# Later route exponentials, freed conditioning steps in the odd mixer, and three u tiles' activations kept in their buffers and used first

## The chip, the cores and the metric

The kernel runs on one core of one Trainium2 chip. The metric is the device time of one execution in microseconds (us). Three runs of the kernel before took 2802.61, 2803.46 and 2820.34 us; their median is 2803.46 us. One further execution was profiled, and all rows below come from it.

The engines are TensorE (PE in the profile; PEld is its weight load), VectorE (DVE), ScalarE (ACT), GpSimd (POOL) and SyncE (SP). DMAs are issued from the queues of SP and ACT.

## The reference, cut to what matters

A first block (stick-breaking attention and a mixture of experts) is followed by two layers of a second block. Layer 0 has the even mixer, layer 1 the odd one; both end in a PEER feed-forward over 16384 single-neuron experts. There are 256 tokens of width 1024.

```python
for layer in range(2):
    mod = (c_act @ ada_w[layer] + ada_b[layer])[:, None, :]
    sh1, sc1, g1, sh2, sc2, g2 = jnp.split(mod, 6, axis=-1)
    h = rmsnorm(x, norm_mix[layer]) * (1.0 + sc1) + sh1
    y = even_mixer(h, ...) if layer % 2 == 0 else odd_mixer(h, ...)
    x = x + g1 * y
    h = rmsnorm(x, norm_ffn[layer]) * (1.0 + sc2) + sh2
    x = x + g2 * peer_ffn(h, ...)

def odd_mixer(h, w_in, b_forget, w_out):          # 16 heads of 64
    q, k, v, f = split_cols(h @ w_in, ODD_SIZES)
    return forgetting_attention(q, k, v, f + b_forget) @ w_out

def peer_ffn(h, w_q, sub_keys, u, v):
    q = (ht @ w_q).reshape(T, 8, 2, 128)
    s = jnp.einsum('thpd,pnd->thpn', q, sub_keys)
    top_s, top_i = lax.top_k(s, 16)
    cand_s = top_s[:, :, 0, :, None] + top_s[:, :, 1, None, :]
    best_s, best_j = lax.top_k(cand_s.reshape(T, 8, -1), 16)
    experts = ...                                  # one of 128 * 128 per pick
    gates = jax.nn.softmax(best_s, axis=-1)
    act = jax.nn.gelu(jnp.einsum('cd,ced->ce', xc, u[ec]))
    return jnp.einsum('ce,ced->cd', gc * act, v[ec])
```

## The kernel before

The kernel doesn't gather experts. In `peer` it multiplies the hidden state with all 16384 rows of u, in 128 tiles of 128 experts (the first product), builds a dense gate matrix G of 128 x 128 x 256, and multiplies the gated activations with all rows of v, again in 128 tiles (the second product). Every fp32 operand is split into a high part (cast by ACT, line 175) and a remainder (subtracted by DVE, line 179, or by POOL, line 181), and each product is three matmuls (`mm3`, lines 216 to 218).

**A u tile** (`act_tile`, with `stream` of line 1261) streams 512 KB of weights in, splits two halves of 512 columns (`puh`, `pul`, three buffers each), runs 24 matmuls into a PSUM bank `u`, and applies the gelu on ACT (line 1273) into a tile `peerA`, of which there are three buffers. `tiles(n)` (line 1278) runs the next n of the 128 tiles and stores each to device memory (`spill`, line 1282, on ACT's queue).

**Routing** (`peer_route`) finds the top 16 per head on DVE, for two halves of the tokens: a long series of maximum and index instructions, then the subtraction of the best score (line 1205), index arithmetic (lines 1208 to 1216), and after the exponentials on ACT (line 1218) the normalisation (lines 1220 to 1222). `tiles(N_EXP)` stands ahead of the exponentials, with N_EXP = 23, and these are ordered behind the last of those gelus by `after(..., k.gelu)`; gelu and exponential use different ACT function tables. `tiles(N_TR)`, with N_TR = 7, stands between normalisation and the transposes (line 1227), which are ordered behind the last of its matmuls. These 30 tiles take their remainders on POOL. The other 98 tiles run among the 64 steps that build G (lines 1294 to 1305) with remainders on DVE.

**The second product** loops over the 128 tiles: it loads the activations back (`get`, line 1310, two tiles ahead), multiplies them with G on DVE (line 1333), splits the result (`pwh`, `pwl`) and the v tile (`pvh`, `pvl`, and `puh`, `pul` for the second half), and accumulates into four PSUM banks `o`. Eight tiles before its end it loads the residual (`xin` into the buffer of `hh`, line 1322).

**Conditioning.** `ada_vec` computes one sixth of a modulation vector as a generator. A step loads part of the weights (`ada` on SP's queue, 1 MB, or `pada` on ACT's queue, 256 KB) and accumulates on DVE (lines 301 and 305). After two steps of the 1 MB kind half a vector is complete; the next step flushes it (`ada_end`: four DVE operations of line 318 for a row, and matmuls of line 325 or 322). `advance(k, n)` runs n steps, `advance(k)` all that are left. In the mixers `load_split` runs `k.bgn` steps, 1 here, each time it fetches a weight block. The odd mixer fetches 13 blocks of `od_in`: one for the forget gate, then for each of four groups of heads q, k and v (`heads`, `heads`, `rows`), and four of `od_out`. Three vectors, twelve steps, belong to it. With `hold=k.norm` the first accumulation of each half vector is ordered behind the norm ahead of the mixer.

The order of instructions on each engine is set when the program is built, by a list scheduler that runs on modelled times: an instruction that is ready in the model while its engine is free can be put ahead of earlier code. At run time every engine takes its instructions in that fixed order.

Of the kernel before, what the change touches and what calls it, by code (L numbers as in the profile page):

```python
# [21 lines left out]
P = 128  # L22
T = 256
# [10 lines left out]
CAP = 64  # L34
EC = 4
EV_QI, EV_KI, EV_CKV, EV_QA, EV_QB, EV_KB, EV_VB = 0, 512, 640, 904, 1416, 1928, 2440
NT = 128
N_EXP, N_TR = 23, 7

CONST = ["anti", "ge", "cum", "m_sb", "m_c"]  # L40
SMALL = [("ident", P), ("iota", P), ("one", P), ("strict", P), ("c1", 8), ("c2", 8), ("ng0", 8), ("ng1", 8), ("nm0", 8), ("nm1", 8),
# [210 lines left out]
class Ahead:  # L252
# [15 lines left out]
    def get(self):  # L268
        if not self.q:
            self.fill()  # L270
        return self.q.popleft()
# [803 lines left out]
def odd_mixer(k, gate):  # L1075
# [3 lines left out]
    with k.tc.tile_pool(name="od", bufs=2, side="right") as pool:  # L1079
# [11 lines left out]
        def rows(g):  # L1091
            proj_rows(k, w, 2 * D + g * 256, 256, v[:, :, g * 256:(g + 1) * 256])
# [24 lines left out]
        nc.vector.tensor_copy(cT, pt[:16, :T])  # L1117
        nc.sync.dma_start(kT[64:65], cT)
        rows(0)
        oT = [one([P, 8, T], f"od_oT{i}", F32R) for i in range(2)]  # L1120
        po = [None]
        for g in range(4):
# [118 lines left out]
def peer(k, l):  # L1241

    nc, a = k.nc, k.a
    spill = k.dram.tile([NT, P, T], F32, name=f"peer_a{l}")
    outer = ExitStack()
    k.pp = outer.enter_context(banks(k, f"p{l}", u=2, o=4))
    acc = [[bank(k, "o") for n in range(2)] for th in range(2)]
    with k.tc.tile_pool(name=f"peer{l}", bufs=2) as pool, k.tc.tile_pool(name=f"pws{l}", bufs=4) as wp:
# [24 lines left out]
            k.gelu = nc.scalar.activation(A, ps[:, :T], AF.Gelu_apprx_tanh)  # L1273
            return A

        left = iter(range(NT))

        def tiles(n, **kw):
            for _ in range(n):
                i = next(left, None)  # L1280
                if i is not None:
                    nc.scalar.dma_start(spill[i], act_tile(i, **kw))

        peer_route(k, l, idx, gates, tiles)
        k.pst.close()
        with k.tc.tile_pool(name=f"peerg{l}", bufs=1, side="right") as gpool:
            G = gpool.tile([P, NT, T], F32, name=f"G{l}")
            rest = NT - N_EXP - N_TR
            for t4 in range(T // 4):
                tiles((t4 + 1) * rest * 4 // T - t4 * rest * 4 // T, lo_eng="dve")  # L1290
                t0 = 4 * t4

                oh = tmp(k, pool, [P, 4, 2, P // 2, 2], "oh", BF16, tag="pvl", bufs=3)
                nc.vector.tensor_tensor(oh.rearrange("p t c i d -> p (t c) i d"), iob[:, None].to_broadcast([P, 8, P // 2, 2]),
                                        idx[:, t0:t0 + 4].rearrange("p t c d -> p (t c) d")[:, :, None, :].to_broadcast([P, 8, P // 2, 2]),
                                        ALU.is_equal)
                og = [tmp(k, pool, [P, 4, P // 2, 2], "og", BF16, tag=g, bufs=3) for g in ("pvh", "pwh", "pwl")]
                for c in range(3):
                    nc.vector.tensor_tensor(og[c], oh[:, :, 0], gates[:, t4, c, :, None, :].to_broadcast([P, 4, P // 2, 2]), ALU.mult)
                pg = bank(k).rearrange("p (t i) -> p t i", t=4)  # L1300
                for j in range(4):
                    for c in range(3):
                        nc.tensor.matmul(pg[:, j], oh[:, j, 1].rearrange("p i d -> p (i d)"), og[c][:, j].rearrange("p i d -> p (i d)"),  # L1303
                                         start=j == 0 and c == 0, stop=True, skip_group_check=True)
                nc.scalar.copy(G[:, :, t0:t0 + 4], pg.rearrange("p t i -> p i t"))
            tiles(NT)

            def get(i):
                A = tmp(k, pool, [P, T], "peerA", bufs=3)
                nc.sync.dma_start(A, spill[i])  # L1310
                return A

            As, vs = deque(), deque()

            xin = k.hh.bitcast(F32).rearrange("p (h c) t -> p h (c t)", h=2)
            gate, k.gb = (k.hl.bitcast(F32)[:, 4 * j:4 * j + 4, :].rearrange("p c t -> p (c t)") for j in range(2))
            for i in range(NT):
                advance(k, 1 - i % 2 if k.bg else 1)
                if i == NT - 8:
                    k.set, k.users = None, [k.gelu]  # L1320
                    preload(k, SETS[AF.Ln])
                    nc.sync.dma_start(xin, k.xd)
                    nc.sync.dma_start(gate, k.gd[l])
                    if l:
                        nc.sync.dma_start(k.gb, k.nfd[0, :].partition_broadcast(P))
                while len(As) < 3 and i + len(As) < NT:
                    As.append(get(i + len(As)))
                    vs.append(stream(a[f"pv{l}"][i + len(vs)]))
                ahead.fill()
                A, v = As.popleft(), vs.popleft()  # L1330

                w = bank(k, "u")[:, :T]
                nc.vector.tensor_mul(w, A, G[:, i, :])
                wh, wl = split(k, pool, w, "pw", bufs=3)
                for n in range(2):

                    vp = split(k, pool, v[:, n * 512:(n + 1) * 512], "pu" if n else "pv", bufs=3)
                    for th in range(2):
                        ts = slice(th * P, (th + 1) * P)
                        mm3(k, acc[th][n], (wh[:, ts], wl[:, ts]), vp, i == 0)  # L1340
            advance(k)
    open_x(k, l + 1)
    if l == 0:
# [44 lines left out]
def program(k, out):  # L1388
# [52 lines left out]
    for l in range(2):  # L1441
        mod = k.mod[l + 1]
        with Section(k, f"m{l}", (4, 6)[l], "right", s=3, t=1, o=2):
# [4 lines left out]
                with norm("m1", "right") as k.nw:  # L1448
                    norm_T(k, k.nm1, mod[:, 8:16], mod[:, 0:8], "s")

            k.bg = [ada_vec(k, l + 1, v, r, hold=k.norm) for v, r in ((2, g1), (4, None), (3, None))]
            k.bgn = 1
            if l:
                nc.sync.dma_start(k.nfd, a["norm_final"][None, :])
            (even_mixer, odd_mixer)[l](k, g1)
# [73 lines left out]
```

## Time and profile before

| What | Value |
|---|---|
| median of three runs | 2803.46 us (2802.61 to 2820.34) |
| the profiled execution, device time | 2797.37 us |
| its span, first to last instruction | 2795.3 us |
| PE busy / DVE busy / ACT busy / POOL busy | 94% / 65% / 45% / 14% |
| mean granted TensorE clock | 0.972 |
| layer 0: routing and first product, second product | about 905 to 1395, 1402 to 1761 us |
| layer 1: odd mixer | about 1775 to 1925 us |
| layer 1: routing and first product, second product | about 1930 to 2422, 2428 to 2780 us |

A row of a timeline gives the start in us, the time in us, the engine, the line, the operation, the tiles written and read, and in brackets how long the engine sat idle before it and what ended that. A granted clock of 1.00 is full speed (2.4 GHz), 0.50 the lower level (1.2 GHz).

### The profile page before, as it was taken

The page shows a single profiled execution, that of the slowest core. Times are in us where ns is not written, and L with a number is a line of the kernel's source. Part 1 is how long each engine was busy: PE and PEld are TensorE (multiplying, and loading weights), DVE is VectorE, ACT ScalarE, POOL GpSimd, SP SyncE. Part 2 cuts the span into 40 slices and gives each one's busy share as a digit, 9 for nine tenths or more (in the row PEclk, how much of TensorE's full clock was granted, in tenths as well). Part 3 has the DMA queues.
Part 4 walks back from the last instruction along what each step waited for, and adds up shares of the span by engine and source line. Part 5 has one row for each costly group of instructions (what it writes and reads, how often), then busy time and mean ns, then how long its engine had stood idle before and what let it go on. Part 6 is the DMA issues. An engine that isn't in the chain of part 4 may idle for free.

```text
span 2795.3 us, 47442 instructions
## 1 busy us (share of the span) xinstructions
PE 2617.3 (94%) x17213; PEld 2138.7 (77%) x17213; DVE 1819.4 (65%) x3977; ACT 1249.5 (45%) x2527; POOL 387.0 (14%) x289
## 2 busy tenths in 40 slices
PE   7998999999798979999999999798979999899998
PEld 5873344444586979999978888688979999888886
DVE  6753111111686698777787887855798777787776
ACT  4531000000445545555545555455445555555554
POOL 2220000000234472000000000224660000000000
PEclk9899999999899999999999999899989999999999
DMA  8578999998562356666798987743356666787775
GB/s 358 217 268 353 421 421 416 419 418 369 209 256 77 123 177 195 202 197 198 220 306 258 298 257 239 292 182 110 127 169 199 198 198 200 258 267 249 242 243 162
DMA packets 208149, 696.53 MB, mean 249 GB/s; under 512 B 23143, under 2 KB 91127, under 8 KB 167588
## 3 DMA queue, kind: packets, MB, share of 16 engines
q1 hardware_dynamic: 161108, 641.51, 65.8%
q10 hardware_dynamic: 46800, 51.93, 5.5%
q8 instruction: 137, 2.24, 0.3%
q14 instruction: 104, 0.85, 0.1%
HBM read 655.55 MB, written 37.78 MB: 248 GB/s over the span
## 4 chain that ended last, share of the span: by engine, by line
PE 59%; DVE 3%; issue 2%; DMA 2%; POOL 1%; ACT 0%; SPq 0%; POOLq 0%; DVEq 0%; ACTq 0%
PE u L216 8%; PE u L218 8%; PE u L217 8%; PE o L218 7%; PE o L217 7%; PE o L216 7%; PE w L1303 3%; PE w L216 2%; PE w L217 2%; PE w L218 2%; DMA pada<-in_ada 1%; POOL pul L181 1%; DVE adaacc L305 1%; PE w L1170 1%; DMA peerA<-peer_a 1%
## 5 line engine op out<-in xcount | busy, mean ns | idle before, releaser
L216 PE MATMUL u<-hh,puh 128*128 128x256 f32 x2048 | 589.0, 288 | 24.2 <-ACT puh L175 24.2
L175 ACT CAST puh<-pst 128x512 fp32r<-128x512 f32 x768 | 476.7, 621 | 296.3 <-PE u L217 285.4
L218 PE MATMUL u<-hh,pul 128*128 128x256 f32 x2048 | 579.3, 283 | 9.4 <-POOL pul L181 9.0
L217 PE MATMUL u<-hl,puh 128*128 128x256 f32 x2048 | 577.8, 282 | 0.0
L179 DVE TENSOR_TENSOR pul<-pst,puh 128x512 fp32r<-128x512 f32 x648 | 444.7, 687 | 157.0 <-ACT puh L175 156.4
L216 PEld LDWEIGHTS u<-hh,puh 128*128 128x128 f32 x2048 | 388.8, 190 | 24.6 <-ACT puh L175 24.6
L218 PEld LDWEIGHTS u<-hh,pul 128*128 128x128 f32 x2048 | 388.1, 190 | 13.1 <-POOL pul L181 12.1
L217 PEld LDWEIGHTS u<-hl,puh 128*128 128x128 f32 x2048 | 389.1, 190 | 0.0
L175 ACT CAST pvh<-pst 128x512 fp32r<-128x512 f32 x256 | 159.2, 622 | 195.2 <-ACT puh L175 118.2
L179 DVE TENSOR_TENSOR pvl<-pst,pvh 128x512 fp32r<-128x512 f32 x256 | 176.6, 690 | 67.0 <-ACT pvh L175 67.0
L181 POOL TENSOR_TENSOR wspl<-wT,wsph 128x512 fp32r<-128x512 f32 (+1 forms) x82 | 113.5, 1386 | 746.2 <-DMA kc<-in_k_consts 492.2
L216 PE MATMUL o<-pvh,pwh 128*128 128x512 f32 x512 | 202.2, 395 | 13.8 <-ACT pwh L175 13.8
L217 PE MATMUL o<-pvl,pwh 128*128 128x512 f32 x512 | 200.9, 392 | 0.6 <-DVE pvl L179 0.5
L218 PE MATMUL o<-pvh,pwl 128*128 128x512 f32 x512 | 200.7, 393 | 0.6 <-DVE pwl L179 0.6
L216 PE MATMUL o<-puh,pwh 128*128 128x512 f32 x512 | 200.1, 391 | 0.0
L217 PE MATMUL o<-pul,pwh 128*128 128x512 f32 x512 | 200.1, 391 | 0.0
L218 PE MATMUL o<-puh,pwl 128*128 128x512 f32 x512 | 199.9, 391 | 0.0
L216 PE MATMUL w<-hh,wsph 128*128 128x256 f32 x648 | 190.9, 295 | 7.4 <-ACT wsph L175 2.9
L218 PE MATMUL w<-hh,wspl 128*128 128x256 f32 x648 | 186.5, 288 | 0.5 <-DVE wspl L179 0.5
L217 PE MATMUL w<-hl,wsph 128*128 128x256 f32 x648 | 186.7, 288 | 0.0
L181 POOL TENSOR_TENSOR pul<-pst,puh 128x512 fp32r<-128x512 f32 x120 | 172.0, 1446 | 61.3 <-ACT puh L175 54.7
L744 DVE TENSOR_TENSOR moesg<-moesg,v 128x512 f32<-128x512 f32 x16 | 11.0, 687 | 223.9 <-PE v L739 223.9
(405 smaller groups left out, 5022.8 us busy)
## 6 DMA issues: line engine op xcount, KB each, us to landing
pst<-in_pu SPq DMA_DIRECT2D x256, 512.0 KB, 4.0
pst<-in_pv SPq DMA_DIRECT2D x256, 512.0 KB, 4.6
moeg<-in_moe_g SPq DMA_DIRECT2D x64, 1024.0 KB, 10.8
moeu<-in_moe_u SPq DMA_DIRECT2D x64, 1024.0 KB, 9.9
moed<-in_moe_d SPq DMA_DIRECT2D x64, 1024.0 KB, 11.9
ada<-in_ada SPq DMA_DIRECT2D x56, 1024.0 KB, 6.7
peer_a<-peerA ACTq DMA_DIRECT2D x256, 128.0 KB, 3.6
peerA<-peer_a SPq DMA_DIRECT2D x256, 128.0 KB, 3.8
```

The costliest lines, as they stand in the source:

```text
L175: ins = nc.scalar.copy(hi, src)
L179: nc.vector.tensor_tensor(lo, src, hi, ALU.subtract)
L181: nc.gpsimd.tensor_tensor(lo, src, hi, ALU.subtract)
L216: mm(out, lhs[0], rhs[0], start=st, stop=True, skip_group_check=True)
L217: mm(out, lhs[0], rhs[1], start=False, stop=True, skip_group_check=True)
L218: k.mm = mm(out, lhs[1], rhs[0], start=False, stop=True, skip_group_check=True)
L305: nc.vector.scalar_tensor_tensor(acc, wt[:, c, :], cond[:, kc, :1], acc, op0=ALU.mult, op1=ALU.add)
L744: nc.vector.tensor_mul(sg, sg, pgu["u"])
L1170: nc.tensor.matmul(ps[:, (2 * th + p) * P:(2 * th + p + 1) * P], qh[:, p, th * P:(th + 1) * P], keys[:, p, :], start=True, stop=True)
L1303: nc.tensor.matmul(pg[:, j], oh[:, j, 1].rearrange("p i d -> p (i d)"), og[c][:, j].rearrange("p i d -> p (i d)"), start=j == 0 and c == 0 ...
```

## The change

Three things are changed. `N_EXP` goes from 23 to 28 in both layers, so that 28 tiles stand ahead of the route exponentials, 7 between them and the transposes, and 93 in the building of G. In layer 1, `k.bgn` is 0 until `rows(0)` is done and 1 from then on, and the conditioning of layer 1 is no longer ordered behind the norm (`hold=None`); layer 0 is as it was. The last three u tiles (`KEEP = 3`) are not stored: their activations stay in the three `peerA` buffers, and the second product takes these three tiles first and the other 125 after them.

```diff
-NT = 128
-N_EXP, N_TR = 23, 7
+NT, KEEP = 128, 3
+N_EXP, N_TR = 28, 7
...
         rows(0)
+        k.bgn = 1
         oT = [one([P, 8, T], f"od_oT{i}", F32R) for i in range(2)]
...
-    spill = k.dram.tile([NT, P, T], F32, name=f"peer_a{l}")
+    spill = k.dram.tile([NT - KEEP, P, T], F32, name=f"peer_a{l}")
...
-        left = iter(range(NT))
+        left, kept = iter(range(NT)), {}
 
         def tiles(n, **kw):
             for _ in range(n):
                 i = next(left, None)
-                if i is not None:
-                    nc.scalar.dma_start(spill[i], act_tile(i, **kw))
+                if i is None:
+                    return
+                A = act_tile(i, **kw)
+                if i < NT - KEEP:
+                    nc.scalar.dma_start(spill[i], A)
+                else:
+                    kept[i] = A
...
+            order = list(range(NT - KEEP, NT)) + list(range(NT - KEEP))
+
             def get(i):
+                if i in kept:
+                    return kept[i]
                 A = tmp(k, pool, [P, T], "peerA", bufs=3)
                 nc.sync.dma_start(A, spill[i])
                 return A
...
-            for i in range(NT):
-                advance(k, 1 - i % 2 if k.bg else 1)
-                if i == NT - 8:
+            for m, i in enumerate(order):
+                advance(k, 1 - m % 2 if k.bg else 1)
+                if m == NT - 8:
...
-                while len(As) < 3 and i + len(As) < NT:
-                    As.append(get(i + len(As)))
-                    vs.append(stream(a[f"pv{l}"][i + len(vs)]))
+                while len(As) < 3 and m + len(As) < NT:
+                    As.append(get(order[m + len(As)]))
+                    vs.append(stream(a[f"pv{l}"][order[m + len(vs)]]))
...
-                        mm3(k, acc[th][n], (wh[:, ts], wl[:, ts]), vp, i == 0)
+                        mm3(k, acc[th][n], (wh[:, ts], wl[:, ts]), vp, m == 0)
...
-            k.bg = [ada_vec(k, l + 1, v, r, hold=k.norm) for v, r in ((2, g1), (4, None), (3, None))]
-            k.bgn = 1
+            k.bg = [ada_vec(k, l + 1, v, r, hold=None if l else k.norm) for v, r in ((2, g1), (4, None), (3, None))]
+            k.bgn = 1 - l
```

## Rows read from the trace of the kernel before

**Rows 1.** The page, part 1: busy time of each engine over the span.

```profile
PE 2617.3 (94%) x17213; PEld 2138.7 (77%) x17213; DVE 1819.4 (65%) x3977; ACT 1249.5 (45%) x2527; POOL 387.0 (14%) x289
```

**Rows 2.** PE's waits: waiter, what for, us in total, times, longest.

```profile
PE u L216 <- ACT puh L175: 24.2, 2, 12.1
...
PE o L216 <- ACT pwh L175: 13.8, 3, 6.8
PE w L325 <- DVE adaacc L318: 11.2, 4, 9.2
```

**Rows 3.** ACT's timeline at the route exponentials of layer 0.

```profile
1028.77 0.38 ACT L1273 ACTIVATE peerA<-u 128x256 f32<-128x256 f32 x1
...
1031.61 0.38 ACT L1273 ACTIVATE peerA<-u 128x256 f32<-128x256 f32 x1
...
1047.43 0.42 ACT L1218 ACTIVATE rows<-rows 128x256 f32<-128x256 f32 x1 [14.14 <-DVE rows L1205]
...
1048.49 1.28 ACT L1273 ACT_TABLE_LOAD   x1
1049.79 0.38 ACT L1273 ACTIVATE peerA<-u 128x256 f32<-128x256 f32 x1
```

**Rows 4.** Windows: busy us and instructions by engine, PEclk, DMA share, GB/s.

```profile
1050.00:1055.00 5.00, 4.76 (x24) 4.76 (x24) 5.00 (x4) 2.14 (x6) 3.09 (x3) 0.55 0.47 159
1150.00:1200.00 50.00, 50.00 (x482) 49.58 (x482) 36.85 (x71) 28.77 (x56) 0.00 (x0) 1.00 0.64 198
```

**Rows 5.** POOL's timeline in the routing of layer 0.

```profile
972.87 61.79 POOL L181 TENSOR_TENSOR pul<-pst,puh 128x512 fp32r<-128x512 f32 x40 [7.88 <-ACT puh L175]
1048.55 1.64 POOL L181 TENSOR_TENSOR pul<-pst,puh 128x512 fp32r<-128x512 f32 x1 [13.89 <-ACT puh L175]
```

**Rows 6.** DVE's timeline in the routing of layer 0.

```profile
989.07 0.40 DVE L1203 MAX8 bv<-c 128x8 f32<-128x256 f32 x1
...
995.42 1.16 DVE L1205 TENSOR_TENSOR rows<-bv 128x128 f32<-128x128 f32 x1
...
1040.97 0.40 DVE L1203 MAX8 bv<-c 128x8 f32<-128x256 f32 x1
...
1047.12 0.27 DVE L1205 TENSOR_TENSOR rows<-bv 128x128 f32<-128x128 f32 x1
...
1063.70 1.50 DVE L1222 TENSOR_TENSOR rows<-rows,gz 128x256 f32<-128x256 f32 x1
```

**Rows 7.** The tile `rows`: duration min/median/max in ns, first and last start.

```profile
L1227 PE MATMUL w<-smalls,rows x12: 270/272/273, 1068.5 to 2095.5; 128*128 128x128 f32 x12
```

**Rows 8.** PE's timeline in the odd mixer.

```profile
1791.11 2.04 PE L325 MATMUL w<-adaacc,smalls 128*128 128x512 f32 x2 [9.22 <-DVE adaacc L318]
```

**Rows 9.** The tile `ada`, 1740 to 1930 us: durations in ns, first and last start.

```profile
L305 DVE SCALAR_TENSOR_TENSOR adaacc<-ada,cond,adaacc x42: 729/748/1789, 1778.9 to 1860.4; 128x512 f32<-128x512 f32 x42
```

**Rows 10.** Windows in the odd mixer, columns as in rows 4.

```profile
1790.00:1795.00 5.00, 3.89 (x12) 2.88 (x13) 4.86 (x13) 0.59 (x1) 0.00 (x0) 0.50 0.93 380
1875.00:1880.00 5.00, 4.96 (x39) 4.56 (x39) 1.12 (x2) 2.82 (x7) 1.85 (x2) 1.00 0.00 0
```

**Rows 11.** DVE's timeline at the start of the second product, layer 0.

```profile
1398.21 0.75 DVE L305 SCALAR_TENSOR_TENSOR adaacc<-pada,cond,adaacc 128x512 f32<-128x512 f32 x1 [3.67 <-DMA pada<-in_ada]
...
1400.59 0.75 DVE L305 SCALAR_TENSOR_TENSOR adaacc<-pada,cond,adaacc 128x512 f32<-128x512 f32 x1 [1.03 <-DMA pada<-in_ada]
1401.26 0.43 DVE L1333 TENSOR_TENSOR u<-peerA,G 128x256 f32<-128x256 f32 x1
```

**Rows 12.** ACT's timeline there: the last copy into G.

```profile
1395.83 0.58 ACT L1305 COPY G<-w 128x512 f32<-128x512 f32 x1
```

**Rows 13.** PE's timeline there: the first matmul of the second product.

```profile
1402.14 0.80 PE L216 MATMUL o<-pvh,pwh 128*128 128x512 f32 x1 [6.76 <-ACT pwh L175]
```

**Rows 14.** SP's queue there: the load of the residual.

```profile
1399.43 0.49 SPq L1322 DMA_DIRECT2D hh<-x_dram  x1
```

**Rows 15.** A window there, columns as in rows 4.

```profile
1400.00:1405.00 5.00, 2.86 (x7) 2.28 (x8) 3.79 (x8) 2.03 (x3) 0.00 (x0) 0.50 1.03 375
```

## The prediction

> **What bounds the kernel now.** I read the page first: TensorE is busy for 94% of the span [rows 1], so time is to be had only where it waits or runs at the lower clock. The view of PE's waits names three places that the change touches [rows 2]. PE waits 12.1 us in each of the two layers for a `puh` of a u tile, which ACT delivers; 6.8 us in each layer for the first `pwh` of the second product (two of the 13.8 us' three waits); and 9.2 us, once, for a conditioning row. Timelines of ACT, DVE and POOL show what lies behind each.
>
> The first is the route exponentials. Gelus come 2.84 us apart (1028.77 to 1031.61) up to the 23rd tile. The next work on ACT is the exponential, and it starts only at 1047.43, after 14.14 us of idleness that DVE's subtraction of line 1205 ended [rows 3]. ACT takes its work in order, so no further u tile can be cast; PE empties its buffers, waits, and comes back at a granted clock of 0.55 [rows 4]. The wait is for DVE's top-k, not for anything that u tiles need. While G is built PE is busy for 50.00 of 50 us, DVE for 36.85 [rows 4]: each tile taken out of that stage gives its full PE time back.
>
> **The change part by part.**
>
> *Five more tiles ahead of the exponentials, each layer.* The 28th gelu should start at 1031.61 + 5 x 2.84 = 1045.8 us and end at 1046.2; the subtraction ended at 1047.12 + 0.27 = 1047.4 [rows 3, 6]. Five tiles thus fit the gap, and the work ahead of them isn't touched. They leave the building of G, worth 5 x 2.84 = 14.2 us there. From PE's side: it gets back 12.1 us of waiting, and what the low clock cost: 24 matmuls in the window from 1050 against 5 / (2.84 / 24) = 42 at full speed, 18 x 0.118 = 2.1 us [rows 2 to 4]. Both counts give 14.2.
>
> Of this some is given back. With exponential and gelu in different tables ACT is held from about 1046.2 to the exponential's end (1047.8), and then by the next table load of 1.28 us. That is 2.9 us at least, against 1.2 us of slack that ACT has in a tile while it works beside PE (busy for 28.77 of 50 us [rows 4], so idle for 42% of 2.84). I take a wait of 1.7 us on PE. It is nothing if the three `puh` buffers cover it, and 3.3 us if the subtraction comes late, as follows.
>
> POOL was idle for 13.89 us in the gap [rows 5] and now works there. The top-k instructions don't notice: the same MAX8 takes 0.40 us with POOL busy (989.07) and idle (1040.97) [rows 5, 6]. The subtraction does: 1.16 us with POOL busy, 0.27 without [rows 6]. So the exponential comes 0.9 us later, and if the four small index operations behind it lose as much each, the normalisation of 1063.70 ends at 1063.7 + 1.5 + 4.5 = 1069.7 in place of 1065.2, an estimate. The transposes start at 1068.5 [rows 7], so they could be late by 1.2 us at most. The value: 14.2 - 1.7 = 12.5 us in each layer, 25 us in both; the bounds in a layer are 14.2 and 14.2 - 3.3 - 1.2 = 9.7. The five extra stores and loads of a tile's weights are the same transfers earlier.
>
> A switch of tables is weighed here. The second load starts at 1048.49 and the gelu at 1049.79, 1.30 us later [rows 3]: the load alone, with no gap behind it. The Trainium skill, "ScalarE: Activation LUTs", section "What ACT_TABLE_LOAD costs", counts 2.66 us for every switch, a load of 1.28 and a drain of 1.38. By that rule two switches hold ACT 2.8 us longer, and the sum would be 5.5 us smaller; the row speaks against the drain.
>
> *The odd mixer's conditioning.* Ahead of `rows(0)` four steps ran, and DVE's accumulations (0.748 us each, 42 of them on line 305 and six that open a half vector on line 301, the last at 1860 [rows 9]) crowded the first weight splits; PE waited 9.22 us for the row to be flushed [rows 8] and came back at 0.50 of the clock, with 12 matmuls in the next window [rows 10], some 12 x 0.118 = 1.4 us more than at full speed (0.118 us a matmul, as above). Without these steps in the way this is 10.6 us. The four steps are 16 accumulations, 12.0 us of DVE, and their four 1 MB loads. They don't vanish: nine steps now go with the nine fetches of groups 1 to 3, where eight went before, and three are left for `advance(k)` ahead of the output product. What hides them is DVE's idleness there: 1.12 of 5 us busy in the window from 1875, DMA share 0.00 while PE works [rows 10]. On SP's queue the weight blocks move ahead of the conditioning loads, so splits start earlier, and the last three loads stand ahead of those of `od_out`, with the idle DMA time from 1875 on to land in. If the cover weren't there, three steps would cost 3 x 4 x 0.748 = 9.0 us at PE's flush. Freeing them from the norm lets the scheduler put an accumulation into the norm's chain: 4 x 0.748 = 3.0 us for a step, or more if its load is late. I take 10.6 less 2.6 for a flush that now meets the softmax of group 0, so 8 us; bounds 10.6 and -1.4 (10.6 - 9.0 - 3.0).
>
> *The three kept tiles.* G's last copy ends at 1395.83 + 0.58 = 1396.4 [rows 12], the first matmul starts at 1402.14 [rows 13]. Of the 5.7 us between, DVE's product of 0.43 [rows 11] and a cast of about as much on ACT need at least 0.8, so at most 4.9 us can be had; the low clock adds at most half of 2.86 us, 1.4 [rows 15]. But DVE's product isn't held by the activations alone: two accumulations stand ahead of it in DVE's order, and each waited for a `pada` load, 3.67 and 1.03 us [rows 11]. Keeping the tiles takes three stores and three loads of 128 KB away, 0.79 MB, or 2.1 us at the 375 GB/s of that window [rows 15]; and it lets SP issue the 1 MB residual load of 1399.43 [rows 14] some 4 us sooner, which shares the DMA engines with the `pada` loads and could make them up to 2.8 us later. Bounds in a layer: a gain of 6.3 and a loss of 2.8. I take the nearest row, the order as it stands with less traffic: 2 us, 4 us in both. Later loads of `peerA` run two tiles ahead as before.
>
> The sum is 25 + 8 + 4 = 37 us. From the profiled execution's 2797.4 us (span 2795.3) that is 2760. The median of the runs is 6.1 us above the profiled time, and I carry that over: 2803.5 - 37 = 2766 us.
>
> **The rivals.**
>
> *Only the routing pays.* The flush meets a busy DVE in group 1, and the first product still waits for the late conditioning loads. For it: DVE's order ahead of that product holds two late loads already [rows 11]. Against it: DVE is idle most of the later odd mixer. 2803.5 - 25 = 2778 us.
>
> *Everything pays in full.* No table wait, the odd mixer's 10.6, and the product moved ahead of both accumulations: 2 x 14.2 + 10.6 + 2 x 6.3 = 51.6, so 2752 us. For it: the scheduler may place the product first, as it is ready when G is. Against it: the same scheduler put the accumulations there.
>
> *The gap doesn't fill.* The change doesn't do what it says in the routing, because POOL at work delays DVE by as much as the tiles take, and the exponential is late again. For it: 1.16 against 0.27 us [rows 6]. Against it: the MAX8s, of which the gap consists, cost the same. Left are 8 + 4 = 12 us: 2791 us.
>
> *Slower: the flush stall repeats.* Twelve steps have six flushes. If each meets DVE as the first did, now among the softmax operations, PE waits 9.22 us six times in place of once, 46 us more, against 29 gained elsewhere: 2803.5 + 17 = 2820 us. It decides from (29 + 9.2) / 6 = 6.4 us a flush on. Against it: of the four waits on line 318 in the whole kernel only one was long, 9.2 of 11.2 us [rows 2].
>
> **How the numbers follow.** The forecast has a chance of 0.55, only the routing 0.20, everything 0.12, the unfilled gap 0.09, the repeated stall 0.04. The predicted time is the forecast's, 2766. 1% of the median, about what a measurement can tell from no change, is 28 us, so faster means below 2775.4. All of "everything" lies there, nine tenths of the forecast, two fifths of "only the routing": 0.12 + 0.50 + 0.08 = 0.70. Slower by over 1% needs flushes of 11 us: 0.03. The rest, 0.27, is within 1%. The range from 2748 to 2792 takes in the first four cases and leaves out the slower one and the tails.
>
> **What would show it.** In the profile after, PE's wait for `puh` should fall from 24.2 to under 6 us, ACT's wait ahead of the exponential from 14 to under 3 us, POOL's subtractions of `pul` rise by 20 with their idle gap gone, and the building of G end some 12 us earlier against its layer's start. The odd mixer's 9.2 us wait should be gone, with later waits for lines 318 and 307 under 3 us in sum. The first matmul of the second product should follow G's last copy by 3 to 4 us in place of 5.7. The prediction is wrong if the exponential still comes late, if the norm of layer 1 gets longer by accumulations put into it, or if the waits turn up again at a flush.

## The result, and the profile after

The changed kernel took 2767.36 us (median of 4 runs, 2761.82 to 2771.66) against 2803.03 us for the kernel before on the same chip: a ratio of 0.986, with a 95% interval from 0.984 to 0.988. The prediction was 2766. The profiled execution has a span of 2760.0 us against 2795.3.

The parts don't add up as they were forecast, though. The table cuts each profiled execution at the same places. A is the time from the first score copy of a peer layer to the end of G's last copy, B from there to the first matmul of the second product, C from that matmul to the first `ybuf`, each for layers 0 / 1. D is the odd mixer's stretch, from layer 0's first `ybuf` to layer 1's first score copy. All marks are starts or ends in the timelines of ACT, PE and DVE.

| kernel | median (us) | ratio to before, interval | A | B | C | D |
|---|---|---|---|---|---|---|
| before | 2803.03 | | 480.2 / 480.1 | 5.7 / 5.8 | 357.8 / 351.6 | 182.8 |
| **changed** | 2767.36 | 0.986 [0.984, 0.988] | 469.8 / 469.0 | 1.4 / 1.4 | 354.4 / 349.8 | 184.0 |
| e1_exp28 | 2781.73 | 0.993 [0.991, 0.995] | 468.2 / 467.9 | 9.1 / 10.1 | 356.8 / 351.4 | 182.3 |
| e2_keep | 2796.73 | 0.997 [0.996, 0.999] | 481.6 / 480.7 | 1.7 / 4.1 | 355.8 / 349.6 | 183.6 |
| e3_odd | 2803.95 | 1.000 [0.999, 1.002] | 480.7 / 480.9 | 6.1 / 6.5 | 359.7 / 350.9 | 182.9 |
| e4_exp_keep | 2767.59 | 0.988 [0.986, 0.990] | 469.4 / 468.8 | 1.4 / 1.4 | 357.9 / 349.9 | 183.6 |
| e5_free | 2763.45 | 0.985 [0.981, 0.989] | 469.1 / 468.0 | 1.4 / 1.4 | 359.7 / 349.9 | 179.6 |
| e6_hold | 2763.72 | 0.985 [0.981, 0.988] | 469.3 / 468.2 | 1.4 / 1.4 | 354.4 / 350.3 | 180.9 |
| e7_nocond | 2750.41 | 0.980 [0.977, 0.983] | 468.9 / 469.3 | 1.4 / 1.4 | 357.4 / 350.3 | 167.9 |
| e8_spread | 2755.20 | 0.982 [0.978, 0.985] | 469.6 / 469.0 | 1.4 / 1.4 | 355.6 / 351.0 | 173.0 |
| e9_exp26 | 2775.70 | 0.991 [0.989, 0.992] | 474.1 / 474.0 | 1.4 / 1.4 | 354.6 / 349.9 | 184.2 |
| e10_keep1 | 2775.87 | 0.991 [0.990, 0.993] | 468.4 / 468.9 | 1.0 / 1.0 | 360.4 / 357.5 | 183.9 |
| e11_late_x | 2774.55 | 0.991 [0.988, 0.994] | 468.4 / 468.3 | 5.3 / 7.6 | 357.4 / 351.2 | 183.0 |
| e12_spread_hold | 2759.14 | 0.984 [0.983, 0.986] | 468.8 / 472.1 | 1.4 / 1.4 | 357.6 / 349.9 | 175.6 |

From before to changed, A falls by 10.5 and 11.1 us, B by 4.4 in each layer, C by 3.3 and 1.9, and D rises by 1.2. That is 34.4 us. Another 0.6 us stand ahead of layer 0's first score copy and 0.3 behind layer 1's first `ybuf`, and the span fell by 35.2. One profile of a kernel is not exact to the us: with the same code A differs by up to 1.5 us between profiles (3 more in e12's layer 1), D by 1.4, and C by 1.4 in layer 1 and by 5.3 in layer 0.

The exponential, in ACT's timeline of the changed kernel (start, us, instruction, and in brackets the idle time before it), answers to [rows 3]:

```profile
1046.23 0.38 ACT L1274 ACTIVATE peerA<-u 128x256 f32<-128x256 f32 x1
1046.62 1.28 ACT L1219 ACT_TABLE_LOAD   x1
...
1047.92 0.42 ACT L1219 ACTIVATE rows<-rows 128x256 f32<-128x256 f32 x1
...
1048.94 1.28 ACT L1274 ACT_TABLE_LOAD   x1
1050.24 0.38 ACT L1274 ACTIVATE peerA<-u 128x256 f32<-128x256 f32 x1
```

The 28th gelu starts at 1046.23 (forecast 1045.8), the exponential 0.5 us after its old place, and no idle time stands before it. Each activation follows its table load by 1.30 us from start to start, both times, as before. The Trainium skill, "ScalarE: Activation LUTs", section "What ACT_TABLE_LOAD costs", adds a drain of 1.38 us; this trace has no gap for one either.

DVE beside it (answers to [rows 6]):

```profile
1045.61 0.43 DVE L1204 MAX8 bv<-c 128x8 f32<-128x256 f32 x1
...
1046.49 1.35 DVE L1206 TENSOR_TENSOR rows<-bv 128x128 f32<-128x128 f32 x1
...
1065.33 1.43 DVE L1223 TENSOR_TENSOR rows<-rows,gz 128x256 f32<-128x256 f32 x1
```

The subtraction takes 1.35 us with POOL at work where it took 0.27 with POOL idle. The last MAX8 takes 0.43, as it did before with POOL idle:

```profile
996.50 1.45 DVE L1208 TENSOR_SCALAR ju<-bj 128x128 uint32<-128x128 uint32 x2
...
1046.24 0.43 DVE L1203 MAX8 bv<-c 128x8 f32<-128x256 f32 x1
...
1047.31 0.35 DVE L1208 TENSOR_SCALAR ju<-bj 128x128 uint32<-128x128 uint32 x2
```

The Trainium skill, "SBUF — State Buffer", section "Who interferes with whom", says that a VectorE instruction with two SBUF inputs contends with a GpSimd instruction that reads SBUF, and that one with a single input, outside the two-port modes, doesn't; the subtraction and MAX8 agree. The two instructions of line 1208 have one input each and took 1.45 us with POOL at work, 0.35 with it idle; in which mode they ran no row shows.

In the page's costliest groups (busy, mean ns, then idle before and its releaser), `puh` no longer holds PE, which waited 24.2 us for it [rows 2], and POOL has 20 subtractions more:

```profile
L216 PE MATMUL u<-hh,puh 128*128 128x256 f32 x2048 | 586.6, 286 | 0.5 <-ACT puh L175 0.5
...
L181 POOL TENSOR_TENSOR pul<-pst,puh 128x512 fp32r<-128x512 f32 x140 | 199.5, 1439 | 35.6 <-ACT puh L175 27.7
```

At the start of layer 0's second product, timelines of DVE and then PE (answers to [rows 11, 13]):

```profile
1383.33 0.75 DVE L305 SCALAR_TENSOR_TENSOR adaacc<-pada,cond,adaacc 128x512 f32<-128x512 f32 x1
1383.99 0.68 DVE L179 TENSOR_TENSOR pul<-pst,puh 128x512 fp32r<-128x512 f32 x1
1385.38 0.77 DVE L1344 TENSOR_TENSOR u<-peerA,G 128x256 f32<-128x256 f32 x2 [0.71 <-ACT G L1311]
...
1388.26 0.75 DVE L305 SCALAR_TENSOR_TENSOR adaacc<-pada,cond,adaacc 128x512 f32<-128x512 f32 x1
```

```profile
1386.71 0.50 PE L216 MATMUL o<-pvh,pwh 128*128 128x512 f32 x1 [3.56 <-ACT pwh L175]
```

The product waits only for G's copy. The next accumulation stands behind it, not ahead of it as before.

The odd mixer, windows from layer 0's first `ybuf` to the first score matmul of layer 1 (length, then each engine's busy time with its instructions, PE's granted clock, DMA share, GB/s), before and after:

```profile
1759.92:1941.79 181.87, 155.89 (x1150) 141.66 (x1149) 121.99 (x256) 100.21 (x236) 59.21 (x42) 0.92 0.51 188
```

```profile
1741.14:1924.18 183.04, 160.21 (x1151) 144.54 (x1150) 122.75 (x255) 100.05 (x236) 57.51 (x41) 0.92 0.51 188
```

PE is idle for 22.8 us where it was for 26.0. But it is busy for 4.3 us more with the same matmuls: part of them ran at the lower clock, at group 3 (below). The mean of 0.92 in both doesn't show it, because before much of the lower clock fell on an idle PE, busy for 4.09 of the 10.20 us from 1785.00 on, at 0.50.

### The profile page after: what moved, and what is told of

It reads as the page before. It is cut to its first block, busy times and chain, and to the rows that moved or that the text cites. A ratio compares the mean times of both kernels' runs of the same rounds, so it can differ in the third digit from the quotient of the medians.

```text
span 2760.0 us, 47425 instructions
## 1 busy us (share of the span) xinstructions
PE 2614.7 (95%) x17213; PEld 2135.7 (77%) x17213; DVE 1810.1 (66%) x3957; ACT 1246.4 (45%) x2527; POOL 414.8 (15%) x309
## 4 chain that ended last, share of the span: by engine, by line
PE 60%; DVE 2%; DMA 2%; issue 1%; POOL 1%; ACT 1%; ACTq 0%; POOLq 0%; DVEq 0%
PE u L216 8%; PE u L218 8%; PE u L217 8%; PE o L216 8%; PE o L217 8%; PE o L218 8%; PE w L1309 3%; PE w L216 2%; PE w L217 2%; PE w L218 2%; POOL pul L181 1%; DMA pada<-in_ada 1%; DVE adaacc L305 1%; PE w L1171 1%; PE o L1078 1%
## 5 line engine op out<-in xcount | busy, mean ns | idle before, releaser
L179 DVE TENSOR_TENSOR pul<-pst,puh 128x512 fp32r<-128x512 f32 x628 | 431.1, 687 | 141.2 <-ACT puh L175 140.6
L181 POOL TENSOR_TENSOR pul<-pst,puh 128x512 fp32r<-128x512 f32 x140 | 199.5, 1439 | 35.6 <-ACT puh L175 27.7
```

Of the source, the lines that this page charges most:

```text
L179: nc.vector.tensor_tensor(lo, src, hi, ALU.subtract)
L181: nc.gpsimd.tensor_tensor(lo, src, hi, ALU.subtract)
```

## The experiments

**Each part by itself, and two together.** Two theories stood against each other: the prediction's split (routing 25 us, odd mixer 8, kept tiles 4), and what the traces seemed to say (routing about 21, kept tiles 10 to 16, odd mixer nothing). D in these four expectations counts to the score matmul, 0.9 us earlier than in the table.

```diff
-N_EXP, N_TR = 23, 7          # kernel before
+N_EXP, N_TR = 28, 7          # e1_exp28: this alone
```

> Only the five more tiles ahead of the exponentials (N_EXP 28); odd mixer and stores as before. By the prediction's split: 12.5 us a layer, so 25 us under the kernel before, about 2778 us, with G's last copy 12.5 us earlier against the layer's start. By the reading of the two traces: G's last copy about 10.5 us earlier in each layer (14.2 less about 3 us in which the last u tiles wait), and the 5.7 us between that copy and the first second-product matmul stay, so about 21 us, 2782 us. If the gain at G's end depended on the kept tiles, under 15 us.

2781.73 us, 19.8 less than the 2801.56 of the kernel before beside it. A falls by 12.0 and 12.2 us, the prediction's 12.5; but B rises from 5.7 to 9.1 and 10.1, so some 3.4 to 4.3 us a layer are given back at once. DVE's and SP's timelines show where:

```profile
1395.88 0.75 DVE L305 SCALAR_TENSOR_TENSOR adaacc<-pada,cond,adaacc 128x512 f32<-128x512 f32 x1 [5.58 <-DMA pada<-in_ada]
...
1397.46 0.75 DVE L305 SCALAR_TENSOR_TENSOR adaacc<-pada,cond,adaacc 128x512 f32<-128x512 f32 x1 [0.23 <-DMA pada<-in_ada]
1398.13 0.76 DVE L1333 TENSOR_TENSOR u<-peerA,G 128x256 f32<-128x256 f32 x2
```

```profile
1387.16 0.33 SPq L1322 DMA_DIRECT2D hh<-x_dram  x1
1390.85 5.99 SPq L1310 DMA_DIRECT2D peerA<-peer_a  x3
```

The product still stands behind two accumulations, and the first now waits 5.58 us for its load. The 1 MB residual load (`hh<-x_dram`) is now issued ahead of the first loads of activations. Before, it came behind them, at 1399.43 [rows 14]:

```profile
1394.75 4.11 SPq L1310 DMA_DIRECT2D peerA<-peer_a  x2
```

```diff
-N_EXP, N_TR = 28, 7          # changed kernel
+N_EXP, N_TR = 23, 7          # e2_keep: kept tiles alone; the odd mixer as before
```

> Only the three kept tiles used first; N_EXP 23 and the odd mixer as before. By the prediction's split: 2 us a layer, 4 in all, 2799 us, with the first second-product matmul 3 to 4 us after G's last copy. By the reading of the traces: 5.73 us between G's last copy and that matmul fall to about 1.4, and the second product gains some 3 us more on its way, so 5 to 8 us a layer, 10 to 16 in all, 2787 to 2793 us. If the early start needs the five tiles as well (their accumulations done earlier), the gap stays over 4 us here and the whole is under 4 us.

2796.73 us, 4.8 less: near the prediction's 4, and not the 10 to 16 of the other theory. B is 1.7 and 4.1. The start is earlier without the five tiles too, but not by as much: DVE's product begins behind an accumulation that waited for its load, 0.90 us in layer 0 and 3.31 in layer 1.

```profile
1403.88 0.75 DVE L305 SCALAR_TENSOR_TENSOR adaacc<-pada,cond,adaacc 128x512 f32<-128x512 f32 x1 [0.90 <-DMA pada<-in_ada]
1404.55 0.76 DVE L1343 TENSOR_TENSOR u<-peerA,G 128x256 f32<-128x256 f32 x2
...
2428.14 0.75 DVE L305 SCALAR_TENSOR_TENSOR adaacc<-pada,cond,adaacc 128x512 f32<-128x512 f32 x1 [3.31 <-DMA pada<-in_ada]
```

```diff
+            k.bg = [... hold=None if l else k.norm ...]   # e3_odd: kernel before with this
+            k.bgn = 1 - l
         rows(0)
+        k.bgn = 1
```

> Only the odd mixer's conditioning steps moved behind rows(0) and freed from the norm. By the prediction's split: 8 us faster, 2795 us, from the end of layer 0's second product to the first score copy of layer 1. By the reading of the traces: that stretch stays at 181.9 us within 3 us (10 us gained by the first softmax group, given back by the fourth), so 2802 to 2806 us; with a loss of more than 3 us a version without this part would beat the changed kernel.

2803.95 us, a ratio of 1.000 with an interval from 0.999 to 1.002. The odd mixer's edit by itself gives nothing.

```diff
-            k.bg = [... hold=None if l else k.norm ...]   # changed kernel
-            k.bgn = 1 - l
+            k.bg = [... hold=k.norm ...]                  # e4_exp_keep: the odd mixer as before
+            k.bgn = 1
-        k.bgn = 1                                         # behind rows(0)
```

> The changed kernel without the odd mixer's part (that one as before). By the prediction's split: 29 us under the kernel before, 2774 us. By the reading of the traces: 34 to 37 us under it, 2766 to 2769 us, the same as the changed kernel within 2 us, with the stretch from layer 0's second product to layer 1's first score copy at 181.9 us as before.

2767.59 us, the changed kernel's time. So all of the gain is in the routing and the kept tiles, and these are worth more together (34.0 us) than apart (19.8 + 4.8 = 24.6): the kept tiles take away what the five tiles give back in B. The intervals of these medians reach some 5 to 7 us to either side, so it is B that shows it: the kept tiles cut it by 16.5 us in both layers together with the five tiles (e1 to e4), and by 5.7 without (before to e2). Added to e1, they are worth 14.1 us.

**The odd mixer's two edits apart, and without the work.** The next four start from the changed kernel.

```diff
-            k.bgn = 1 - l                 # changed kernel
+            k.bgn = 1                     # e5_free: steps from the start, but free of the norm
-        k.bgn = 1                         # behind rows(0)
```

> The changed kernel with the odd mixer's steps starting before rows(0) again, but free of the norm (hold gone). If the 9.2 us wait at the first flush came of the place of the steps, it comes back and the first group maximum of the softmax stands at +54 us after layer 0's ybuf; if it came of the hold (accumulations kept back until the norm is done, then all at once), the accumulations run earlier, the wait is under 3 us and the first maximum stands near +46. The stretch from ybuf to layer 1's first score copy: 183 to 185 us in the first case, 176 to 179 in the second.

D is 179.6 us, 4.4 less. The first group maximum stands at +50.3, between the two marks that were given, and the 9.2 us wait is gone although the steps are at their old place. So the place of the steps doesn't make that wait by itself.

```diff
-            hold=None if l else k.norm    # changed kernel
+            hold=k.norm                   # e6_hold
```

> The changed kernel with the hold kept and only the steps moved behind rows(0). If the accumulations that now run inside the norm cost what the transposes come later (15.85 to 16.80 us after ybuf), the stretch is 1 us shorter than the changed kernel's 184.0, 183 us, 2766 us in all; if the hold was what crowded the first splits, the 9.2 us wait comes back and the stretch is over 188 us.

D is 180.9 us and the wait stays away as well: the hold doesn't make it by itself either, it took both. Either edit by itself brings D down by 2 to 3 us against before, in one profile each; both together, as in the change, bring it back up. The two transposes of the forget gate, which end the first piece of work behind the norm (line 474), start at +15.85 us from the first `ybuf` in the kernel before, at +16.09 here and at +16.80 in the changed kernel, so the forecast loss in the norm is under 1 us. (In e5, whose accumulations begin ahead of the norm, they start at +18.80; how much of that the accumulations cause isn't separated.)

```diff
+            if l:                         # e7_nocond: changed kernel without the odd mixer's conditioning
+                k.bg = []
+                nc.gpsimd.memset(g1, 0.5)
+                nc.gpsimd.memset(mod[:, 24:40], 0.5)
```

> The odd mixer's three conditioning vectors are left out (two constants stand for their values), so this measures what all of that work costs in the stretch. If the early gain is given back later because accumulations and flushes meet the softmax of the later groups, the stretch falls from 184.0 to about 170 us, the last two gaps between group maxima to before's 26.5 and 51 less some, and the kernel to about 2754 us. If the stretch is set by something else (weights, the clock), it stays over 180 us.

D is 167.9 us: this work costs 16 us in the changed kernel, although DVE and the DMA engines had idle time for all of it. The forget gate's transposes stand at +16.85 here, with no accumulation at all, so it isn't the accumulations that make them 1 us later than before.

```diff
             if g:                         # changed kernel
+                k.bgn = 2                 # e8_spread: two steps at a group's first fetch
                 heads(qT, 0, g, 0.125)
+                k.bgn = 1
                 heads(kT, D, g, 1.0)
```

> The changed kernel with two steps at the first fetch of each of groups 1 to 3, so that all twelve go with fetches and none is left for the advance ahead of the output product. If the steps left over are what costs the end (group 3's maxima to the first score copy, 54.6 us against 50.9 in the kernel before), the stretch falls by 3 to 4 us, to about 180; if accumulations cost wherever they stand, it stays at 184 or rises by up to 3.

D is 173.0 us, 11 less than in the changed kernel, and more than was expected. The marks inside D (first softmax maximum of a group, DVE line 840, from the first `ybuf`):

| kernel | group 0 | to group 1 | to group 2 | to group 3 | to the first score copy | D |
|---|---|---|---|---|---|---|
| before | 54.4 | 23.0 | 27.1 | 26.5 | 51.8 | 182.8 |
| changed | 43.8 | 26.3 | 27.5 | 30.8 | 55.6 | 184.0 |
| e5_free | 50.3 | 24.6 | 27.1 | 26.6 | 51.0 | 179.6 |
| e6_hold | 43.4 | 25.4 | 27.2 | 30.8 | 54.1 | 180.9 |
| e7_nocond | 44.3 | 21.2 | 25.7 | 25.7 | 51.0 | 167.9 |
| e8_spread | 44.2 | 21.7 | 28.2 | 27.9 | 51.0 | 173.0 |
| e12_spread_hold | 44.8 | 23.5 | 28.2 | 27.8 | 51.3 | 175.6 |

In the changed kernel the first group is 10.6 us earlier, as forecast. Then 3.3 us are lost up to group 1, 4.3 between groups 2 and 3, and 3.8 behind group 3. Of the 48 accumulations (lines 301 and 305) the changed kernel runs 12 ahead of group 0's maxima, 12 between groups 0 and 1, 8 between 1 and 2, 16 between 2 and 3 and none behind; the kernel before has 28, 10, 10, 0 and 0, and e8 16, 8, 16, 8 and 0. The last ones ahead of groups 1 and 3 start 0.7 us before the maxima in the changed kernel, 8 and 13 us before them in e8. So two of the losses stand where more accumulations than before run right up to the maxima. (The kernel before runs its 10 up to group 1's maxima too, and its 23.0 us there lie between e8's 21.7 and the changed kernel's 26.3.) DVE's timeline at group 3's start in the changed kernel, and ACT's row behind it:

```profile
1863.88 3.36 DVE L305 SCALAR_TENSOR_TENSOR adaacc<-ada,cond,adaacc 128x512 f32<-128x512 f32 x3
1867.16 1.77 DVE L179 TENSOR_TENSOR wspl<-wO,wsph 128x512 fp32r<-128x512 f32 x1
1868.85 0.74 DVE L305 SCALAR_TENSOR_TENSOR adaacc<-ada,cond,adaacc 128x512 f32<-128x512 f32 x1
1869.51 1.33 DVE L840 TENSOR_REDUCE smm<-s 128x1 f32<-128x128 f32 x5
```

```profile
1870.22 0.37 ACT L241 ACTIVATE ebd<-s,smm 128x128 f32<-128x128 f32 x1 [3.18 <-DVE smm L840]
```

The last accumulations and a split stand ahead of the maxima, and ACT waits 3.18 us for these. In e8 it is DVE that waits there, for PE's scores:

```profile
1865.16 0.62 DVE L840 TENSOR_REDUCE smm<-s 128x1 f32<-128x128 f32 x2 [0.86 <-PE s L822]
```

What is lost behind group 3, where no accumulation is left, is PE's clock. In the changed kernel two flushes (line 322) stand ahead of the scores of the group's last head, the second behind a wait of 0.58 us, and from about 1869.6 to 1879.8 us the granted clock is 0.50:

```profile
1868.15 1.00 PE L322 MATMUL w<-smalls,adaacc 128*128 128x1 f32 x8
1869.74 1.84 PE L322 MATMUL w<-smalls,adaacc 128*128 128x1 f32 x8 [0.58 <-DVE adaacc L305]
```

```profile
1869.60:1879.80 10.20, 9.50 (x35) 7.21 (x36) 4.72 (x22) 4.54 (x19) 0.00 (x0) 0.50 0.00 0
```

In e8 one flush stands there, and the clock stays at 1.00. The 12 us from the first maximum of group 3 on, in the changed kernel, then in the kernel before, then in e8 behind the window of its whole stretch:

```profile
1869.50:1881.50 12.00, 11.16 (x46) 8.46 (x46) 5.24 (x24) 5.24 (x20) 0.00 (x0) 0.57 0.00 0
```

```profile
1890.90:1902.90 12.00, 11.97 (x84) 9.77 (x83) 5.96 (x23) 7.56 (x25) 1.95 (x2) 1.00 0.01 1
```

```profile
1743.14:1915.20 172.06, 154.35 (x1151) 140.62 (x1150) 118.10 (x255) 100.46 (x236) 57.90 (x41) 0.95 0.53 199
1865.10:1877.10 12.00, 11.97 (x84) 9.76 (x83) 5.96 (x23) 7.56 (x25) 1.93 (x2) 1.00 0.01 1
```

From that mark on PE does 46 matmuls in 12 us at 0.57 of the clock, and 84 at full clock in the other two. The 9.50 us that it is busy at half the clock would be 4.75 at full, an estimate that fits the 3.8 us lost against before and the 4.6 against e8. Whether the flushes, the held-up softmax or both brought the clock down isn't shown. Over the stretch e8 has 17.7 us of idle PE (22.8 in the changed kernel) and 154.4 us of busy PE (160.2). Without the conditioning it is

```profile
1743.74:1911.00 167.26, 149.05 (x1117) 137.11 (x1116) 83.38 (x194) 99.53 (x234) 57.20 (x42) 0.95 0.36 130
```

with 18.2 us of idle and 149.1 of busy PE. So e8 is left with hardly more than PE's own part in the rows, 34 matmuls and 5.3 us. It is the best of these versions that compute everything: 2755.20 us, 0.982 of before (0.978 to 0.985), against 0.986 (0.984 to 0.988) for the change. The two intervals, each against its own runs of the kernel before, just overlap; that e8 is faster than the change rests on D, 173.0 against 182.9 to 184.2 in the four profiles with the change's odd mixer.

**Sizes and causes at the second product's start.**

```diff
-N_EXP, N_TR = 28, 7          # changed kernel
+N_EXP, N_TR = 26, 7          # e9_exp26
```

> The changed kernel with 26 tiles ahead of the exponentials in place of 28. If each tile is worth its own time, G's last copy comes 2 x 2.84 = 5.7 us later against the layer's start in each layer (469.5 becomes 475), 11 us in all, about 2778 us. If two tiles' worth of the wait is covered by the buffers between PE and ACT, the loss is under 3 us a layer.

A rises by 4.4 and 5.0 us against the changed kernel's profile, and by 5.1 and 5.4 against the means of the profiles with 28 tiles (469.0 and 468.6, layer 1 without e12): 2.2 to 2.7 us a tile where 2.84 was counted, so little of each is covered, if any. PE's waits from 900 to 1420 us show it (us, times, longest); in the changed kernel this wait is 0.5:

```profile
PE u L216 <- ACT puh L175: 3.6, 1, 3.6
```

```diff
-NT, KEEP = 128, 3            # changed kernel
+NT, KEEP = 128, 1            # e10_keep1
```

> The changed kernel with one kept tile in place of three. If what counts is that the first product needs no load, so that DVE takes it right after G's copy, the first second-product matmul still follows G's last copy by about 1.4 us and PE meets the second tile's load a tile later: a loss of up to 3 us a layer. If what counts is the traffic and the buffers of three tiles, the gap is 4 us or more, and the loss 3 to 8 us a layer.

Each theory had one half right. B is 1.0 us: one kept tile is enough for the first product to go ahead. But C is 7.7 us longer in layer 1 (in layer 0 some 4 against the mean of the other profiles with kept tiles), because the stall comes back a tile later. PE's timeline, and DVE's behind it:

```profile
1386.01 0.79 PE L216 MATMUL o<-pvh,pwh 128*128 128x512 f32 x1 [3.25 <-ACT pwh L175]
...
1391.80 0.80 PE L218 MATMUL o<-pvh,pwl 128*128 128x512 f32 x1 [4.14 <-DVE pwl L179]
```

```profile
1390.05 0.75 DVE L305 SCALAR_TENSOR_TENSOR adaacc<-pada,cond,adaacc 128x512 f32<-128x512 f32 x1 [4.50 <-DMA pada<-in_ada]
1390.72 0.68 DVE L179 TENSOR_TENSOR pul<-pst,puh 128x512 fp32r<-128x512 f32 x1
1391.32 0.42 DVE L179 TENSOR_TENSOR pwl<-u,pwh 128x256 fp32r<-128x256 f32 x1
```

The split `pwl` that PE needs stands behind an accumulation that waits for its load. The lower clock adds to it: from the first of these matmuls on PE is at 0.50 for 9.6 us, where the changed kernel ran this start of layer 0 at full clock.

```profile
1386.00:1395.60 9.60, 5.45 (x12) 3.89 (x13) 4.51 (x10) 2.17 (x3) 0.00 (x0) 0.50 0.86 307
```

```diff
-                nc.sync.dma_start(A, spill[i])            # e1
+                k.pa = nc.sync.dma_start(A, spill[i])     # e11_late_x: e1 with this
-                    nc.sync.dma_start(xin, k.xd)
+                    xl = nc.sync.dma_start(xin, k.xd)
+                    after(k, xl, k.pa)
```

> The 28 tiles without kept ones, and the 1 MB residual load put behind the last loads of kept activations in SP's queue, late in the second product, in place of ahead of the first of them. If the 9.1 and 10.1 us between G's last copy and the first second-product matmul come of accumulations whose loads share the DMA engines with that load, the gap falls to 4 to 6 us, 8 to 10 us in all, about 2772 us. If they come of the first activations' way through DRAM alone (store, then load), the gap stays at 8 or more.

B falls from 9.1 to 5.3 and from 10.1 to 7.6 us. In layer 0 that is all that the five tiles had added, in layer 1 somewhat over half of it. The residual load's place is a cause, but in layer 1 not the only one. There an accumulation ahead of the product still waits 3.42 us for its load, and another load, of 512 KB (`hl<-nf_dram`, which layer 0 doesn't have), now stands ahead of the first loads of activations, where e1 had it behind them (at 2418.69, the loads from 2407.82 on). It may hold layer 1 as the residual load did; no run moves it, so that stays open. SP's queue and DVE in e11:

```profile
2397.19 0.33 SPq L1326 DMA_DIRECT2D hl<-nf_dram  x1
2397.62 3.73 SPq L1310 DMA_DIRECT2D peerA<-peer_a  x2
```

```profile
2404.95 0.75 DVE L305 SCALAR_TENSOR_TENSOR adaacc<-pada,cond,adaacc 128x512 f32<-128x512 f32 x1 [3.42 <-DMA pada<-in_ada]
```

The kept tiles reach 1.4 in both layers.

```diff
-            hold=None if l else k.norm    # e8_spread
+            hold=k.norm                   # e12_spread_hold
```

> Two steps at the first fetch of each of groups 1 to 3, as in the spread version, and the hold on the norm kept as in the kernel before. If both gains add (3 us by the hold, 11 by the spread), the stretch from layer 0's ybuf to layer 1's first score copy is 170 to 171 us and the kernel at 2752; if the spread alone took the gain, it stays at 173 and about 2755. Without any conditioning it was 167.9, so less than that isn't to be had.

D is 175.6 us: the hold adds nothing to the spread steps, and in this one profile costs 2.6. Layer 1's A is 3 us longer here than in the others, with the same code there. PE waits once 2.1 us for a `pul` of DVE in that stretch, 0.2 in e8; why that split is late isn't explained.

## Why the prediction was right, and where its steps were not

*What bounds the kernel.* This held: PE is busy for 95% of the span, and what the change took away was its waiting: its idle time fell from 178.0 to 145.3 us, its busy time just from 2617.3 to 2614.7.

*Five more tiles ahead of the exponentials: 12.5 us a layer, bounds 9.7 to 14.2.* Right: 12.0 and 12.2 alone (e1), 10.5 and 11.1 in the changed kernel's profile, 11.9 and 12.0 between the means of all profiles with 23 tiles (480.9 and 480.6) and with 28. The exponential came at once, the price of POOL on DVE's subtraction was as forecast (1.35 against 1.16 us), and the normalisation ended at 1066.8, before the transposes of 1068.6. The 1.7 us taken for the table switch show as no wait of that size: PE's waits for `puh` sum to 0.5 us, and those for POOL's remainders rise from 4.7 to 5.4 us in layer 0 (960 to 1080 us). What the step left out is what the earlier end of G meets. Read as the time to the second product's first matmul, the five tiles alone gain just 8.6 and 7.9 us.

*The odd mixer: 8 us.* Wrong: D didn't fall. It is 183.7 us as the mean of the four profiles with this edit (changed, e3, e9, e10), and 183.1 of the five without (before, e1, e2, e4, e11). The 10.6 us from the lost wait were sized right, to the first softmax group. The term that failed is the 2.6 us for a flush that meets the softmax, for which the prediction has no row, together with the cover named for the moved steps, idle DVE time near 1875: the three leftover steps and the ninth didn't use that idleness. Their 16 accumulations fell between groups 2 and 3, where they held up maxima and exponentials, and beside their last flushes PE ran at half the clock for 10.2 us. Of the bounds, 10.6 and -1.4, the lower one was where it ended. The loss in the norm chain, 3.0 us at the bound, was at most 1 in the change, and not by accumulations (e7).

*The kept tiles: 2 us a layer, bounds -2.8 and 6.3.* Too small. B fell by 4.4 in each layer, close to the 4.9 that were named as the most; C by 1.5 and 1.2 more, taking the means over the profiles with three kept tiles and without (356.4 and 357.9; 350.1 and 351.3), so some 5.6 in layer 1. In layer 0, where C runs from 354.4 to 359.7 with kept tiles and from 356.8 to 359.7 without, its 1.5 us are not clear of the scatter. The step that failed is "the order as it stands": the product did not stay behind two late accumulations. With nothing to load for it, it is placed right behind G's copy. The trace of before could not show this order; the rival "everything pays in full" had named it, and had it right for this part. The prediction also put the earlier residual load down to the kept tiles; e1 and e11 show that it is the five tiles that bring it forward, and the kept tiles that make it harmless.

*The sum.* 37 us forecast, 35.7 measured. By the means over profiles it is 1.2 us less by the routing (23.8 for 25), 8.7 less by the odd mixer and 7.5 more by the kept tiles, so 34.6; what is missing to 35.7 is less than profiles of the same code differ by. The total was right by luck, through errors that cancel. Of the signs named, `puh`, the exponential, POOL's 20 subtractions and the lost 9.2 us wait came as forecast. G's end was 11 in place of 12 us earlier, and the first matmul 1.4 us after G's copy in place of 3 to 4. The later waits for lines 318 and 307 were small, as said, which shows how little that sign was worth: the loss was in the softmax and in the clock.

## What to carry to other kernels

An edit that removes a named wait is only worth what is left at the end of its stage: mark the stage at several points, and see where the gain is handed back. Background work is not free just because its engine is idle on average; ask which instruction of the critical chain stands behind it in the same engine's order, and spread it so that none is left over where that chain is tight. Two edits can be worth much more together than apart, when one brings a stage's end forward and the other takes away what it then runs into.

## What the runs showed of the hardware that was not expected

The granted clock after nearly the same pause is not always the same. In the changed kernel's layer 0 PE waits 3.56 us for the first `pwh` and comes back at full clock; in e4 it waits 3.54 us for it and comes back at half (1.2 GHz), and so it does in the changed kernel's own layer 1 after 3.36 us (0.50 from 2395.46 to 2398.46). The first 5 us of the second product, changed and then e4:

```profile
1386.70:1391.70 5.00, 4.99 (x22) 4.15 (x23) 3.45 (x9) 3.01 (x6) 0.00 (x0) 1.00 1.01 349
```

```profile
1388.50:1393.50 5.00, 4.96 (x12) 3.90 (x13) 3.21 (x9) 2.43 (x4) 0.00 (x0) 0.50 0.99 367
```

Ten matmuls fewer, at 0.23 us each (22 in 5 us), are 2.3 us, two thirds of the 3.4 us by which C differs between these two in layer 0. What decides it the runs don't show.
